# Conditioning products of a four-layer sequence kernel: from split fp32r weights in four columns to unsplit fp32 weights in four column quarters

## The chip, the cores and the metric

The kernel runs on one core of a Trainium2 chip. The metric is device time in microseconds (us) for one execution; the median of three runs before the change is 2190.75 us (2190.43 to 2190.81).

## The reference, cut to what matters

Four blocks transform a sequence of 512 latent tokens with 1024 channels (and, in the first two, 256 context tokens). Before each of the first two layers the input is modulated: a conditioning vector is multiplied by a large weight, and the 3072 results are the layer's shift, scale and gate for each channel. There is one such vector for the latents and one for the context, so the product has only two columns on one side:

```
s = silu(c)                       # [2, 1024]: latents and context
mod = s @ w_ada[l] + b_ada[l]     # [2, 3072], l = 0, 1
shift, scale, gate = split(mod, 3)
h = x * (1 + scale) + shift       # what layer l projects
x = layer_norm(alpha * x + gate * y)
```

Everything else (window attention with a convolution branch in layer 0, a gated linear recurrence in layer 1, then two more blocks with feed-forward networks) is left alone by the change.

## The kernel before

**Layout.** Channels lie on the 128 partitions, in eight tiles; tokens run along the free dimension. A weight is loaded in blocks of 128 x 1024 fp32 (512 KB, all eight k tiles of 128 output channels) by SP's DMA queue into a buffer tagged `r`. ScalarE copies it into a rounded fp32r part `h` (L244), and VectorE or GpSimd subtracts that to get the remainder `l` (L250). A product of a block takes three matmuls for each k tile (L313): high by high, low by high, high by low.

**The conditioning (`conditioning`, `ada`).** The weight `wada` has 2 x 12 chunks of 1 MB. Chunk i below 8 gives shift and scale of channel tile i, chunks 8 to 11 the gates of two tiles each. A chunk comes as two halves (j = 0, 1), each 128 x 1024 with four k tiles of 256 output columns. Here the weight is what *moves* through the array (256 columns at a time) and the conditioning vector `sc` is what stands in it: four columns, latents and context, each in a high and a low part. Each half is split like any other weight, into `h` by ScalarE and `l` by GpSimd (or, in the first stage, by VectorE for j = 1). Then 16 fp32r matmuls (8 k tiles, h and l) add into four partitions of half a PSUM bank. ScalarE copies the 4 x 256 result to `adat_t`; two transposes through the identity (L434) bring it to 128 partitions; VectorE adds the bias and then the low part's result into `mod`.

**First stage, 0 to about 76 us (`layer0`).** For each of the eight channel tiles k: chunk k + 1 is started, chunk k is finished, the input tile x is loaded and modulated on VectorE (`st_g`, two instructions), split into `a_h` (ScalarE) and `a_l` (VectorE), and TensorE runs this tile's products with the first three blocks of `w_ab`. The pool `st` has four `r`, three `h` and three `l` buffers for the chunks. Beside it VectorE and GpSimd prepare the parameters of a later state-space block (`s5_prepare`, tiles `s5t_*` and `s_*`), which a scheduler mixes in by priority.

**Second stage, about 76 to 388 us (`layer0_mix`).** 24 steps of attention (`attend`), each with a block product of `w_ab` woven in, and from `more_ada` one conditioning chunk in each of 16 steps. These halves take their buffers from the common pool `wp`: three `r`, four `h`, four `l`. The last eight chunks' results are layer 1's.

A scheduler orders every engine's instructions when the program is built; each engine then runs its own list strictly in that order. SP's list holds all DMA issues.

Of the kernel before, what the change touches and what calls it, by code (L numbers as in the profile page):

```python
# [10 lines left out]
F32 = mybir.dt.float32  # L11
# [15 lines left out]
# ---------------------------------------------------------------- host layout  # L27


def _blocks(w, kt=None):  # L30
    """[K, M] -> [M/128, 128, K/128 * 128]: block m holds, per partition, all k tiles of 128 columns."""
    k, m = w.shape
    return np.ascontiguousarray(
        w.reshape(k // 128, 128, m // 128, 128).transpose(2, 1, 0, 3).reshape(m // 128, 128, k)
    )


def _col(v):
    """[n*128] -> [128, n]."""
    return np.ascontiguousarray(np.asarray(v).reshape(-1, 128).T)  # L40


def _pair_heads(n):
    """Column order that puts heads j and 4 + j of 64 dims into one tile of 128."""
    return np.concatenate([np.r_[j * 64:(j + 1) * 64, (4 + j) * 64:(5 + j) * 64] for j in range(n // 128)])


def _constants():
    """Tables that depend on shapes alone."""
# [24 lines left out]
    c["steps"] = np.broadcast_to(np.concatenate([np.arange(9), 8 * np.arange(64)]), (128, 73))  # L74
    dm = np.zeros((128, 16))
# [93 lines left out]
# ---------------------------------------------------------------- the program  # L169


class Alloc:
    """A pool of tiles by tag: tags[tag] = (number of buffers, elements per partition)."""
# [14 lines left out]
class Prog:  # L188
    def __init__(self, es, tc, I, off):
# [3 lines left out]
        self.adat = Alloc(es, tc, "adat", {"t": (2, 256)})  # L193
# [26 lines left out]
    def psum(self, **tags):  # L220
        """Shares out the eight banks by tag: those used longest ago first."""
# [20 lines left out]
    # element by element -----------------------------------------------------  # L242
# [25 lines left out]
    # weights ---------------------------------------------------------------  # L268
    def weights(self, ap, n=1024, eng=None, pool=None):
        """A block of a weight, split exactly into two parts of 12 bits."""  # L270
# [17 lines left out]
    def product(self, out, w, xs, cols, k0=0, ks=None):  # L288
        """out = w.T @ x over the k tiles (or some of them), each operand in two parts."""
# [9 lines left out]
    def firsts(self, ps, blocks, xs, tags=("mm",) * 3):  # L299
        """The latents' products of a layer's first blocks in two halves: of three of them tile by tile of xs as these  # L300
        come, then of the others."""
# [13 lines left out]
    # scores of two heads of 64 dims: both parts of a head's queries fill the rows, so that two passes take  # L315
    # (high, low) by high and high by low
# [22 lines left out]
    def out_products(self, ps, block, xs, parts, use, done, keep=3, n=1024, late=(), begun=None, spare=(None, 0)):  # L339
        """The products for all eight tiles of channels; use(m, bank, tokens) takes each. The last `keep` tiles  # L340
        go part by part, done(tokens) follows when all channels of a part are there. The last of xs come late, by these
        numbers; begun: weights and banks of the first three tiles, done up to there."""
# [36 lines left out]
    def rsqrt(self, r0, t, var, eps):  # L379
        """r0 = 1 / sqrt(var + eps), t is scratch: the table's value and one step of Newton's."""  # L380
# [6 lines left out]
    def rsqrt_table(self, p):  # L387
        """Has the table of rsqrt in place from p's time on."""
        self.act(self.dummy, p[:, 0:1], ACT.Abs_reciprocal_sqrt, bias=self.bias[1e-5])
    # conditioning ----------------------------------------------------------  # L390
    def conditioning(self):
# [5 lines left out]
        self.sc = self.const.tile([128, KT, 4], F32R, name="sc")  # L397
        tv = t.rearrange("p (a b) -> p a b", b=2)
        self.copy(self.sc[:, :, 0:2], tv)
        self.sub(self.sc[:, :, 2:4], tv, self.sc[:, :, 0:2].bitcast(F32))  # L400
# [8 lines left out]
    def ada(self, l, i, p, pool=None):  # L409
        """Chunk i of layer l's shift, scale (plus 1) and gate: the shift and scale of channel tile i, or the gates  # L410
        of two tiles; each of the factors in two parts. p: half a bank."""
        for j in range(2):
            eng = self.nc.vector if pool and j else self.nc.gpsimd
            hi, lo = self.weights(self.I["wada"][l * 12 + i][:, j * 1024:(j + 1) * 1024], eng=eng, pool=pool)
            for k in range(4):
                for w in (hi, lo):
                    self.matmul(
                        p[0:4, :], self.sc[:, 4 * j + k, :], w[:, k * 256:(k + 1) * 256], j + k == 0 and w is hi,
                        j == 1 and k == 3 and w is lo,
                    )  # L420

        def copied():
            t = self.adat("t")[0:4, :]
            self.copy(t, p[0:4, :])
            return t
# [3 lines left out]
        def finish(t=t):  # L429
            t = copied() if t is None else t  # L430
            m = slice(i, 16, 8) if i < 8 else slice(2 * i, 2 * i + 2)
            o = p[:, 0:8].rearrange("p (a b c) -> p a b c", a=2, b=2)
            for a in range(2):
                self.nc.tensor.transpose(p[:, 4 * a:4 * a + 4], t[:, a * 128:(a + 1) * 128], self.idn[0:4, 0:4])  # L434
            md = self.mods[l][:, m, :]
            self.add(md, o[:, :, 0], self.bada[:, l, m, :])
            self.add(md, md, o[:, :, 1])
# [3 lines left out]
    # layer 0 ---------------------------------------------------------------  # L441
    def layer0(self, stop=False):
        """Leaves layer 1's modulated inputs in self.a1 and its residual in DRAM."""
        nc, tc = self.nc, self.tc
        mod = self.mods[0]
        with ExitStack() as es:
            a0 = Alloc(es, tc, "a0", {"h": (8, LT), "l": (8, LT)})
# [3 lines left out]
            with ExitStack() as e1:  # L451
                prep = self.s5_open(e3, e1)
                st = Alloc(e1, tc, "st", {"r": (4, 1024), "h": (3, 1024), "l": (3, 1024), "x": (4, LT), "g": (2, LT)})
# [43 lines left out]
            # layer 0's affine map and layer 1's modulation in one  # L497
# [27 lines left out]
    def layer0_mix(self, es, e0, late, xs, Y, first, s5):  # L525
# [33 lines left out]
        def gate(m, pool):  # L559
            """Twice silu."""  # L560
# [30 lines left out]
        def attend(qT, j, n, ctx, y, sg):  # L591
            """Both heads j and 4 + j for one block of 128 queries."""
# [95 lines left out]
        def conv(i):  # L688
            """The four products of a tile of the convolution's channels, one at each step."""
# [57 lines left out]
    def deepnorm(self, N, ps, xr, mod, emit):  # L747
        """xr + gate * out normalized over channels, without the affine map; emit(k, tokens, tile) takes it."""
# [42 lines left out]
    # layer 1 ---------------------------------------------------------------  # L791
    def lower_bounds(self):
        """The gates' lower bounds, and one less them: the softmax over the one layer, its cumulative sum less the
        first term."""
# [44 lines left out]
    def layer1_mix(self, es, K, xs, Y):  # L839
# [13 lines left out]
        def proj(m, ctx):  # L853
            """A product in two steps; returns its banks."""
# [17 lines left out]
        def mixed(t, m, j):  # L872
            """Of [128, n, 2]: token s at index j + (bit of s, by m)."""
            return pattern(t, j, [[4 * m, t.shape[1] // (2 * m)], [2 * m + 1 - 2 * j, 2], [2, m]])

        def across(t, nb, j):
            """Of [128, 2 nb, 2]: the other of each pair, at the same indices."""
            return pattern(t, 2 + j, [[4, nb], [-1 - 2 * j, 2]])

        def project(h):  # L880
            """The head's queries, forget terms and values."""
# [35 lines left out]
        def scan(h):  # L917
# [7 lines left out]
            # the diagonal of the scores, both ways  # L925
# [4 lines left out]
            # the decay of the context's keys  # L930
# [30 lines left out]
            for l in range(7):  # L961
                m = 1 << l
                nb = L // (2 * m)
                # keys of the halves before and after, queries of the others: by the token's bit l
# [14 lines left out]
                # the state from the context  # L979
# [8 lines left out]
            # the states block by block  # L988
# [43 lines left out]
    # the second block ------------------------------------------------------  # L1032
# [833 lines left out]
```

## Time and profile before

| | us |
|---|---|
| median of three runs | 2190.75 |
| the profiled execution, span | 2191.0 |
| TensorE (PE) busy | 2067.3 (94%) |
| VectorE (DVE) busy | 1418.2 (65%) |
| ScalarE (ACT) busy | 953.2 (44%) |
| GpSimd (POOL) busy | 533.7 (24%) |
| SP queue, DMA share of 16 engines | 28.9% |

The profiled execution's span is within 0.3 us of the median. PE's busy time counts a matmul until its result has drained, and matmuls overlap in that; so 94% is not 94% of what PE could do, and the distance between two *starts* in the timeline is what a matmul costs in a row of others. PEclk is the share of its full clock that TensorE was granted.

### The profile page before, as it was taken

Reading aid. Unit: us, or ns where it says so; the run is one execution under the profiler, and the core shown is the slowest. Engines: PE = TensorE matmul, PEld = TensorE weight load, DVE = VectorE, ACT = ScalarE, POOL = GpSimd, SP = SyncE. Lnnn points to the kernel's source line nnn. Section 1 sums busy time; section 2 is a strip of 40 time slices with the busy share of each in tenths; the row PEclk is TensorE's granted clock in tenths of the full one; section 3 lists DMA queues with packets and bytes.
Section 4 is the critical chain, followed back from the end, with each engine's and each line's share of the span. In section 5 each row is a group of like instructions: output and inputs, shape, how many; then the busy total and the mean of one; then the engine's idle time right before and its main releaser. Section 6 shows DMA issues by size and latency. Waiting matters only on the chain.

```text
span 2191.0 us, 29958 instructions
## 1 busy us (share of the span) xinstructions
PE 2067.3 (94%) x11576; PEld 1760.7 (80%) x11576; DVE 1418.2 (65%) x2322; ACT 953.2 (44%) x1681; POOL 533.7 (24%) x442
## 2 busy tenths in 40 slices
PE   5888999999999999998999999999989799999997
PEld 3677878888888888888778888888887588888886
DVE  9885656578666666688665763544579877354455
ACT  4564444345534444435656443222355645322231
POOL 4343433135322222214111320100142333010011
PEclk9999999999999999999998999999999899999998
DMA  7443334132211111133441223332312232323231
GB/s 232 146 141 118 111 113 123 61 121 77 68 49 59 48 49 49 50 115 106 140 126 40 86 86 107 96 97 96 115 39 87 77 106 64 101 96 104 91 108 44
DMA packets 79998, 204.97 MB, mean 94 GB/s; under 512 B 19056, under 2 KB 28016, under 8 KB 79856
## 3 DMA queue, kind: packets, MB, share of 16 engines
q1 hardware_dynamic: 79856, 203.06, 28.9%
q8 instruction: 91, 1.49, 0.3%
q14 instruction: 51, 0.42, 0.1%
HBM read 188.87 MB, written 14.16 MB: 93 GB/s over the span
## 4 chain that ended last, share of the span: by engine, by line
PE 71%; DVE 17%; issue 5%; ACT 4%; POOL 1%; DMA 0%; POOLq 0%; DVEq 0%; SPq 0%; ACTq 0%
PE mm L313 54%; PE a L313 5%; PE mc L313 3%; PE x L313 2%; DVE wp_l L250 1%; DVE res_x L266 1%; PE s L313 1%; PE S L313 1%; PE o L313 1%; ACT wp_h L244 1%; DVE o_a L266 1%; DVE n_a L250 1%; PE z L313 1%; DVE o_xc L266 1%; DVE o_tr L250 1%
## 5 line engine op out<-in xcount | busy, mean ns | idle before, releaser
L244 ACT ACTIVATE wp_h<-wp_r 128x1024 fp32r<-128x1024 f32 (+1 forms) x295 | 303.8, 1039 | 495.3 <-PE mm L313 256.1
L250 DVE TENSOR_TENSOR wp_l<-wp_r,wp_h 128x1024 fp32r<-128x1024 f32 (+1 forms) x236 | 335.1, 1423 | 105.9 <-ACT wp_h L244 105.9
L313 PE MATMUL mm<-act_h,wp_l 128*128 128x512 f32 (+1 forms) x1008 | 379.1, 376 | 12.0 <-DVE wp_l L250 10.2
L313 PE MATMUL mm<-act_h,wp_h 128*128 128x512 f32 (+1 forms) x1008 | 379.8, 377 | 3.3 <-DVE o_xb L250 1.6
L313 PE MATMUL mm<-act_l,wp_h 128*128 128x512 f32 (+1 forms) x1008 | 379.2, 376 | 3.1 <-POOL act_l L250 3.1
L313 PE MATMUL mm<-a_h,wp_h 128*128 128x512 f32 (+1 forms) x920 | 338.8, 369 | 0.4 <-ACT a_h L244 0.4
L313 PE MATMUL mm<-a_l,wp_h 128*128 128x512 f32 (+1 forms) x920 | 331.6, 361 | 1.6 <-DVE a_l L250 1.5
L313 PE MATMUL mm<-a_h,wp_l 128*128 128x512 f32 (+1 forms) x920 | 331.7, 361 | 0.0
L313 PEld LDWEIGHTS mm<-act_h,wp_l 128*128 128x128 f32 x1008 | 193.1, 192 | 46.0 <-DVE wp_l L250 11.1
L313 PEld LDWEIGHTS mm<-act_l,wp_h 128*128 128x128 f32 x1008 | 193.3, 192 | 37.1 <-POOL act_l L250 4.0
L313 PEld LDWEIGHTS mm<-act_h,wp_h 128*128 128x128 f32 x1008 | 193.3, 192 | 37.0 <-ACT wp_h L244 3.8
L250 POOL TENSOR_TENSOR wp_l<-wp_r,wp_h 128x1024 fp32r<-128x1024 f32 x59 | 151.5, 2576 | 225.0 <-ACT wp_h L244 206.8
L313 PEld LDWEIGHTS mm<-a_l,wp_h 128*128 128x128 f32 x920 | 176.3, 192 | 25.9 <-DVE a_l L250 3.3
L250 POOL TENSOR_TENSOR g_g<-g_g,g_u 128x512 f32<-128x512 f32 x44 | 62.2, 1416 | 548.2 <-DVE g_u L250 501.8
L313 PEld LDWEIGHTS mm<-a_h,wp_h 128*128 128x128 f32 x920 | 176.1, 192 | 23.9 <-issue 2.3
L313 PEld LDWEIGHTS mm<-a_h,wp_l 128*128 128x128 f32 x920 | 176.1, 191 | 23.6 <-issue 0.7
L313 PE MATMUL mm<-h_l,wp_h 128*128 128x512 f32 (+1 forms) x344 | 129.2, 376 | 0.6 <-DVE h_l L250 0.5
L313 PE MATMUL mm<-h_h,wp_h 128*128 128x512 f32 (+1 forms) x344 | 129.0, 375 | 0.3 <-ACT h_h L244 0.3
L313 PE MATMUL mm<-h_h,wp_l 128*128 128x512 f32 (+1 forms) x344 | 128.8, 374 | 0.0
L250 DVE TENSOR_TENSOR g_u<-mm,res_rr 128x512 f32<-128x512 f32 x44 | 30.4, 690 | 123.3 <-PE mm L313 123.3
L244 ACT ACTIVATE m_km<-m_k 128x512 f32<-128x512 f32 x56 | 37.6, 672 | 122.7 <-DVE m_k L250 101.0
L313 PEld LDWEIGHTS mm<-h_l,wp_h 128*128 128x128 f32 x344 | 64.8, 188 | 13.6 <-DVE h_l L250 2.1
(505 smaller groups left out, 4117.6 us busy)
## 6 DMA issues: line engine op xcount, KB each, us to landing
wp_r<-w_gu SPq DMA_DIRECT2D x88, 512.0 KB, 3.5
wp_r<-w_c SPq DMA_DIRECT2D x40, 512.0 KB, 3.5
wp_r<-wada SPq DMA_DIRECT2D x32, 512.0 KB, 3.7
wp_r<-w_d SPq DMA_DIRECT2D x32, 512.0 KB, 3.5
wp_r<-w_ab SPq DMA_DIRECT2D x26, 512.0 KB, 4.5
st_r<-wada SPq DMA_DIRECT2D x16, 512.0 KB, 5.5
wp_r<-w_od SPq DMA_DIRECT2D x16, 512.0 KB, 3.5
s_d<-s_s SPq DMA_DIRECT2D x24, 256.0 KB, 2.8
```

The lines of the kernel that those rows point to most:

```text
L244: self.nc.scalar.activation(out=out, in_=in_, func=ACT.Copy, scale=scale)
L250: (eng or self.nc.vector).tensor_tensor(out=out, in0=a, in1=b, op=op)
L266: self.nc.vector.scalar_tensor_tensor(out=out, in0=a, scalar=s, in1=b, op0=op0, op1=op1)
L313: self.nc.tensor.matmul(out=out, lhsT=a, rhs=b, start=start, stop=stop)
```

## The change

`sc` becomes 128 x 8 x 32 fp32: the two vectors unsplit, and 30 columns of zeros. A chunk's weights are no longer split: the raw fp32 half moves. Of the four k tiles in a half, tile k goes through columns 32k to 32k + 31 of the array and adds into partitions 32k to 32k + 31 of the bank, so that a chunk takes 8 fp32 matmuls: two in each quarter, the second accumulating on the first. ScalarE now copies 128 x 256. Two fp32 matmuls with a 0/1 matrix `sel` (128 x 2, ones where the partition's number modulo 32 is 0 or 1) take the place of the transposes: they turn the result and sum the four quarters. One add of the bias remains. The pool `st` has six `r` buffers and no `h`, `l`. `conditioning` moved into `layer0`, so that its tiles are freed with the layer.

```diff
-        self.sc = self.const.tile([128, KT, 4], F32R, name="sc")
+        self.sc = cond.tile([128, KT, 32], F32, name="sc")
+        self.nc.gpsimd.memset(self.sc, 0.0)
         tv = t.rearrange("p (a b) -> p a b", b=2)
-        self.copy(self.sc[:, :, 0:2], tv)
-        self.sub(self.sc[:, :, 2:4], tv, self.sc[:, :, 0:2].bitcast(F32))
+        self.nc.vector.tensor_copy(out=self.sc[:, :, 0:2], in_=tv)
+        self.sel = cond.tile([128, 2], F32, name="sel")
+        self.nc.sync.dma_start(out=self.sel, in_=self.I["sel"])
...
     def ada(self, l, i, p, pool=None):
+        raw = []
         for j in range(2):
-            eng = self.nc.vector if pool and j else self.nc.gpsimd
-            hi, lo = self.weights(self.I["wada"][l * 12 + i][:, j * 1024:(j + 1) * 1024], eng=eng, pool=pool)
+            t = (pool or self.wp)("r")
+            self.nc.sync.dma_start(out=t, in_=self.I["wada"][l * 12 + i][:, j * 1024:(j + 1) * 1024])
+            raw.append(t)
+        for j in range(2):
             for k in range(4):
-                for w in (hi, lo):
-                    self.matmul(
-                        p[0:4, :], self.sc[:, 4 * j + k, :], w[:, k * 256:(k + 1) * 256], j + k == 0 and w is hi,
-                        j == 1 and k == 3 and w is lo,
-                    )
+                self.nc.tensor.matmul(
+                    out=p[32 * k:32 * k + 32, :], lhsT=self.sc[:, 4 * j + k, :],
+                    rhs=raw[j][:, k * 256:(k + 1) * 256], start=j == 0, stop=j == 1, tile_position=(0, 32 * k),
+                )
...
-            t = self.adat("t")[0:4, :]
-            self.copy(t, p[0:4, :])
+            t = self.adat("t")
+            self.copy(t, p)
...
-            o = p[:, 0:8].rearrange("p (a b c) -> p a b c", a=2, b=2)
+            o = p[:, 0:4].rearrange("p (a c) -> p a c", a=2)
             for a in range(2):
-                self.nc.tensor.transpose(p[:, 4 * a:4 * a + 4], t[:, a * 128:(a + 1) * 128], self.idn[0:4, 0:4])
-            md = self.mods[l][:, m, :]
-            self.add(md, o[:, :, 0], self.bada[:, l, m, :])
-            self.add(md, md, o[:, :, 1])
+                self.matmul(o[:, a], t[:, a * 128:(a + 1) * 128], self.sel)
+            self.add(self.mods[l][:, m, :], o, self.bada[:, l, m, :])
...
-                st = Alloc(e1, tc, "st", {"r": (4, 1024), "h": (3, 1024), "l": (3, 1024), "x": (4, LT), "g": (2, LT)})
+                st = Alloc(e1, tc, "st", {"r": (6, 1024), "x": (4, LT), "g": (2, LT)})
```

TensorE, first stage, before: the end of the second chunk's run and the start of the next (`st_h`, `st_l` are a half's two parts, `t` the half bank, `mm` and `c` products of `w_ab`).

```order
L313 MATMUL t<-st_h,sc 4x256
L313 MATMUL t<-st_l,sc 4x256
L434 MATMUL t<-idn,adat_t 128x4 x2
L313 MATMUL t<-st_h,sc 4x256
L313 MATMUL mm<-a_h,wp_h 128x512
L313 MATMUL t<-st_l,sc 4x256
```

TensorE, the start of its list now:

```order
L425 MATMUL t<-st_r,sc 32x256 x8
L313 MATMUL t<-sel,adat_t 128x2 x2
L425 MATMUL t<-st_r,sc 32x256 x8
L313 MATMUL t<-sel,adat_t 128x2 x2
L313 MATMUL mm<-a_h,wp_h 128x512
L313 MATMUL mm<-a_l,wp_h 128x512
L313 MATMUL c<-a_h,wp_h 128x256
```

The first two chunks now stand whole at the head of the list, straight behind their loads; from the third on each half is a run of four between the products of earlier tiles.

GpSimd, first stage, before: subtractions of half chunks (`st_l`) between those products of the parameter preparation that run there (`s_w`).

```order
L1183 MEMSET s5t_z 128x128
L250 TENSOR_TENSOR st_l<-st_r,st_h 128x1024 x2
L250 TENSOR_TENSOR s_w<-s5t_u,s5t_steps 128x288
L250 TENSOR_TENSOR st_l<-st_r,st_h 128x1024 x3
L250 TENSOR_TENSOR s_w<-s5t_w,s5t_t 128x512
```

GpSimd, the same place now:

```order
L1190 MEMSET s5t_z 128x128
L250 TENSOR_TENSOR s_w<-s5t_u,s5t_steps 128x288
L250 TENSOR_TENSOR s_w<-s5t_w,s5t_t 128x512 x2
L250 TENSOR_TENSOR s_w<-s5t_u,s5t_steps 128x512
L250 TENSOR_TENSOR m_sh<-m_sh,m_sin 128x512
```

The eight subtractions are gone, and the first work of the second stage (`m_sh`) stands right behind the preparation's.

SP's DMA list in the second stage with what each issue waits for, before (`w_ab` a block of the layer's weight, `wada` a half chunk; the names in brackets are semaphores of the DMA queues and of the engine that releases the buffer):

```order
L273 DMA wp_r<-wada 128x1024 [waits DMAHW5_49,Pool_49]
L273 DMA wp_r<-wada 128x1024 [waits Pool_49]
L273 DMA wp_r<-w_ab 128x1024 [waits DMAHW7_49,DMAHW3_49,DVE_49]
L1268 DMA rope_d<-s5t_w 128x512 [waits DMAHW0_49,DVE_49]
L1267 DMA rope_d<-s5t_w 128x512 [waits DMAHW1_49,Activation_49]
```

SP's list now, at the same step:

```order
L421 DMA wp_r<-wada 128x1024 [waits DMAHW6_49,DMAHW2_49,DVE_49]
L421 DMA wp_r<-wada 128x1024 [waits DMAHW7_49,PE_49]
L273 DMA wp_r<-w_ab 128x1024 [waits DMAHW1_49,DMAHW0_49,PE_49]
L1278 DMA s_d<-s_s 128x512 [waits DVE_49]
L1278 DMA s_d<-s_s 128x512 [waits Activation_49]
```

A raw buffer that held a half chunk used to be released by GpSimd's subtraction; it is now released by TensorE's matmuls on it, and the next block of `w_ab` waits for that. Behind about 388 us the instructions of every engine stand in the same order as before.

More of the change, by code (lines that the diff above doesn't have):

```diff
@@ L74, in _constants @@
     c["steps"] = np.broadcast_to(np.concatenate([np.arange(9), 8 * np.arange(64)]), (128, 73))
+    c["sel"] = np.tile(np.eye(32, 2), (4, 1))
     dm = np.zeros((128, 16))
@@ L192, in __init__ @@
         self.const = es.enter_context(tc.tile_pool(name="const", bufs=1))
-        self.adat = Alloc(es, tc, "adat", {"t": (2, 256)})
         self.wp = Alloc(es, tc, "wp", {"r": (3, 1024), "h": (4, 1024), "l": (4, 1024)})
@@ L389, in rsqrt_table, with conditioning @@
         self.act(self.dummy, p[:, 0:1], ACT.Abs_reciprocal_sqrt, bias=self.bias[1e-5])
-    def conditioning(self):
+    def conditioning(self, es):
+        cond = es.enter_context(self.tc.tile_pool(name="cond", bufs=1))
+        self.adat = Alloc(es, self.tc, "adat", {"t": (2, 256)})
         cv = self.vec("cvec")
@@ L444, in layer0 @@
         nc, tc = self.nc, self.tc
-        mod = self.mods[0]
         with ExitStack() as es:
+            self.conditioning(es)
+            mod = self.mods[0]
             a0 = Alloc(es, tc, "a0", {"h": (8, LT), "l": (8, LT)})
@@ L1815, in dump @@
                 result(k, X)
-        P.conditioning()
         if start == 0:
```

## Prediction

> **What bounds the kernel now.** First the windows, cut where the work changes: first stage, second, and the rest, whose order the change leaves alone. Columns: length, busy time of PE, PEld, DVE, ACT and POOL, granted clock, DMA share, GB/s.
>
> ```profile
> 0.00:76.00 76.00, 50.12 (x278) 33.72 (x279) 67.10 (x165) 34.40 (x50) 27.03 (x28) 1.00 0.67 222
> 76.00:388.00 312.00, 281.33 (x1828) 239.75 (x1826) 215.43 (x468) 154.13 (x333) 119.71 (x80) 0.96 0.38 119
> 388.00:2191.00 1803.00, 1735.85 (x9475) 1487.20 (x9474) 1135.68 (x1690) 764.70 (x1300) 386.92 (x334) 0.98 0.26 84
> ```
>
> Only the first 388 of 2191 us can change. In the first stage VectorE is busy 67.1 of 76 us; in the second TensorE is the bound, idle 30.7 of 312, and a mean clock of 0.96 says that it ran at half for some 25 us, worth 12 more. Second view, what TensorE waited for: three rows of the first stage, three of the second (total, times, longest).
>
> ```profile
> PE t L313 <- ACT st_h L244: 12.4, 3, 10.6
> PE t L313 <- DVE st_l L250: 6.5, 5, 2.0
> PE t L313 <- POOL st_l L250: 4.8, 4, 2.1
> ...
> PE x L313 <- DVE m_T L647: 14.4, 5, 4.0
> PE pt L588 <- ACT m_q L244: 5.4, 1, 5.4
> PE pt L654 <- DVE m_T L647: 5.3, 5, 1.3
> ```
>
> First it waits for the splitting of `wada`, later for copies, 25.1 us in these three. Why VectorE is late there shows in the timeline: POOL's subtractions of two half chunks, and VectorE at that time.
>
> ```profile
> 147.80 5.92 POOL L250 TENSOR_TENSOR wp_l<-wp_r,wp_h 128x1024 fp32r<-128x1024 f32 x2
> ...
> 151.38 2.36 DVE L250 TENSOR_TENSOR m_st<-m_st 128x2 f32<-128x2 f32 x1
> ...
> 154.33 0.16 DVE L250 TENSOR_TENSOR m_st<-vecs,m_st 128x2 f32<-128x2 f32 x1
> ```
>
> An operation on two columns takes 2.36 us beside POOL's and 0.16 after it: VectorE stood still for 2.2.
>
> **Part 1: the splitting goes.** The subtractions of the first stage (count, ns min/median/max), and the window of stage two on `wp_l` alone (PE, PEld, DVE, POOL):
>
> ```profile
> L250 POOL TENSOR_TENSOR st_l<-st_r,st_h x8: 2354/2492/3227, 10.6 to 59.9; 128x1024 fp32r<-128x1024 f32 x8
> L250 DVE TENSOR_TENSOR st_l<-st_r,st_h x8: 1210/1218/3372, 13.4 to 65.4; 128x1024 fp32r<-128x1024 f32 x8
> ...
> 76.00:388.00 312.00, 138.20 (x436) 71.52 (x436) 34.58 (x21) 81.24 (x32) 0.96 0.38 119
> ```
>
> In stage one VectorE loses 8 subtractions (about 12 us) and up to 8 x 2.2 us of standing still: 67 falls to 38. In stage two POOL loses 81 of 120 us, and VectorE up to 32 x 2.2 = 70 of 215. That is worth only the waiting above and the half clock that follows pauses: bounds 0 and 25 + 12 = 37 us. I take 20, over half, because VectorE then has much slack but products still wait for chains of softmax steps.
>
> **Part 2: the matmuls.** One chunk in the TensorE timeline, its first, second and last matmul and what follows:
>
> ```profile
> 145.24 0.28 PE L313 MATMUL mc<-wp_h,sc 128*4 128x256 f32 x1 [1.79 <-DVE mod L250]
> 145.36 0.28 PE L313 MATMUL mc<-wp_l,sc 128*4 128x256 f32 x1
> ...
> 146.96 0.28 PE L313 MATMUL mc<-wp_l,sc 128*4 128x256 f32 x1
> 147.07 0.60 PE L644 MATMUL pt<-idn,m_P 128*128 128x128 f32 x4
> ```
>
> A start every 0.115 us, a chunk 1.83 us. No row has an fp32 matmul in a column quarter; the nearest is fp32 in the whole array with 512 columns:
>
> ```profile
> 1272.36 1.02 PE L313 MATMUL z<-res_acc,ones 128*128 128x512 f32 x2
> 1272.82 0.79 PE L313 MATMUL mm<-act_h,wp_h 128*128 128x512 f32 x1
> 1273.45 0.39 PE L313 MATMUL mm<-act_l,wp_h 128*128 128x512 f32 x1
> ```
>
> The program has one matmul there and the trace two records: fp32 runs as two passes, one behind the other. The next fp32r product needs 0.23 us and ends about 1273.45, so the two took 0.86: 0.43 for 512 columns, 0.215 for 256. A chunk now has 16 such passes. Bounds: all in a row 16 x 0.215 = 3.44 us; all four quarters at once 4 x 0.215 = 0.86. Between them: TensorE's records start in the order of the list, so the second pass of a quarter, which needs the same columns as the first, stands ahead of the next quarter's first pass; only second and next first overlap. Eight matmuls then take 9 x 0.215 = 1.94 us, in two runs of four 2.15. I take this value: it is what two passes in one quarter and starts in order give, if quarters are independent at all. The Trainium skill ("TensorEngine Tiling (Array Packing)", Key Properties) speaks against the change: switching the tiling mode drains TensorE. Here the 4-column matmul at 146.96 is followed by a full-width one 0.11 us later, so no drain is seen in this trace. By the rule, with a drain estimated as the 0.28 us of a matmul less its 0.115, stage two's 16 chunks would lose two each, 5 us, and the sum would be 2172; by the row it is nothing, and the sum stays with the row.
>
> The turn: the transposes before, and small fp32 matmuls with a 128-column weight, the nearest to the two with `sel` (four records).
>
> ```profile
> 49.90 0.28 PE L434 MATMUL t<-idn,adat_t 4*128 4x4 f32 x2
> 50.11 0.39 PE L313 MATMUL c<-a_h,wp_h 128*128 128x256 f32 x1
> ...
> 150.04 1.45 PE L313 MATMUL x<-m_vn,m_T 128*128 128x64 f32 x12
> 151.29 0.48 PE L313 MATMUL mm<-a_h,wp_l 128*128 128x512 f32 x1
> ```
>
> 0.21 us becomes 4 x 1.25 / 12 = 0.42. A chunk thus costs TensorE +0.32 us (+1.82 in a row, -0.76 at once), in stage two 16 times: +5 (+29, -12). With the 20 us of part 1: **stage two -15 us**.
>
> **Part 3: the first stage.** Its landmarks: both halves of the first chunk landed, the first `mod`, first and last `a_h`; a chunk's matmuls early on; the DMA at its best; one tile's products with one block.
>
> ```profile
> 9.45 1.06 ACT L244 ACTIVATE st_h<-st_r 128x1024 fp32r<-128x1024 f32 x1 [1.06 <-DMA st_r<-wada]
> 10.73 1.06 ACT L244 ACTIVATE st_h<-st_r 128x1024 fp32r<-128x1024 f32 x1 [0.22 <-DMA st_r<-wada]
> ...
> 24.88 0.83 ACT L244 ACTIVATE a_h<-st_g 128x768 fp32r<-128x768 f32 x1
> ...
> 66.97 0.84 ACT L244 ACTIVATE a_h<-st_g 128x768 fp32r<-128x768 f32 x1 [2.00 <-DVE st_g L263]
> ...
> 22.11 0.15 DVE L250 TENSOR_TENSOR mod<-mod,t 128x4 f32<-128x4 f32 x1
> ...
> 13.17 0.42 PE L313 MATMUL t<-st_h,sc 128*4 128x256 f32 x1
> 13.38 0.42 PE L313 MATMUL t<-st_l,sc 128*4 128x256 f32 x1
> ...
> 12.00:16.00 4.00, 1.87 (x8) 0.86 (x8) 4.00 (x4) 2.34 (x2) 3.45 (x2) 1.00 1.00 387
> ...
> 70.57 0.69 PE mm L313 x3
> 71.25 0.35 PE c L313 x3
> ```
>
> Early TensorE starts one pass per 0.21 us, half speed. Now the first chunk's passes begin at 9.45: two runs of 5 x 0.43 end at 13.8; copy 0.4, `sel` 0.8, add 0.2: `mod` at 15.2 instead of 22.3, **-7 us**. From then on a tile takes (66.97 - 24.88) / 7 = 6.0 us. New floors per tile: DMA 1.44 MB at 387 GB/s 3.7 us; VectorE 38 / 8 = 4.8; TensorE three blocks x (0.69 + 0.35) + 2.15 + 0.42 = 5.7. TensorE sets the pace, and the seven tiles gain 7 x 0.3 = **2 us**. The tail behind the last `a_h` stays. Stage one: **-9 us**.
>
> **What is moved at no cost.** In stage two a buffer of `wada` is now released by TensorE, and the next `w_ab` block and SP's stores queue behind that wait. Cover: between that chunk and the block's first product TensorE's list holds 27,700 columns or more, at 0.115 us per 256 over 12 us.
>
> ```profile
> wp_r<-w_ab SPq DMA_DIRECT2D x26, 512.0 KB, 4.5
> L244 ACT ACTIVATE wp_h<-wp_r 128x1024 fp32r<-128x1024 f32 (+1 forms) x295 | 303.8, 1039 | 495.3 <-PE mm L313 256.1
> L250 DVE TENSOR_TENSOR wp_l<-wp_r,wp_h 128x1024 fp32r<-128x1024 f32 (+1 forms) x236 | 335.1, 1423 | 105.9 <-ACT wp_h L244 105.9
> ```
>
> Landing 4.5, copy 1.0 and subtraction 1.4 need 7; without cover a step would lose the difference. The wider copy of `adat_t` has the same 256 columns per partition; memset, `sel` load and `sc` copy lie ahead of the first landing.
>
> **Sum.** -9 - 15 = -24 us on the profiled 2191.0, which is the median within 0.3: **2167 us**. A measurement here can tell 0.2%, 4.4 us, from no change.
>
> **Rivals.**
> - *Slower: quarters wait for each other.* If the array takes one fp32 pass at a time whatever its columns, a chunk costs 3.44 us. Stage two: +29 - 20 = +9. Stage one: first `mod` 16 x 0.43 + 1.4 after 9.45, at 17.7, -4; the pace is 3.1 + 3.4 + 0.4 = 7.0 us, +7; together +3. **2203 us.** For it: no row shows two matmuls streaming at once. Against: nothing in the trace either, since all matmuls of before that are 32 columns wide stand in the same quarter. It decides from about 3 us per chunk on, where the total crosses zero.
> - *Faster: all four at once.* If a quarter's second pass waits without holding up the others, a chunk takes 0.86 us. Stage two -12 - 20 = -32; stage one: `mod` at 14, -8, then VectorE's 4.8 us is the pace, -9. **2142 us.** The Trainium skill ("TensorE: Matmul & The Clock Gate", Part 3) gives starts about 4 ns apart for matmuls in different tiles and 2.38 times the rate for three column tiles, and also says that matmuls start and end strictly in order; no run here shows either for fp32.
> - *VectorE's freedom buys little.* Stage two's waits may be the softmax chain itself: then 20 shrinks towards 0 and my forecast becomes 2187. This is inside the range.
>
> **How the numbers follow.** Overlap by halves 0.47, in a row 0.31, all at once 0.22. The range reaches from the fast case with a few us more of part 1 to the slow one with a few us less: **2138 to 2206**, about 0.1 outside at each end. The forecast's own range is 2154 to 2189. Faster by over 0.2%: 0.45 + 0.22 + 0.03 = 0.70; within: 0.06; slower: 0.24.
>
> **What would show it.** Starts of the eight records' pairs in a chunk: every 0.215 us in a row (16 starts over 3.4 us), in pairs (1.9), or nearly together (0.9). VectorE's 2.36 us rows gone, m_T waits below 10 us, first `mod` near 15 us, last `a_h` near 58. The prediction is wrong if a chunk takes over 3 us, if waits of `mm` for `wp_l` or `wp_h` appear in stage two, or if the time behind stage two changes by more than 3 us.

## The result, and the profile after

The changed kernel takes 2130.2 us (median of four runs, 2128.3 to 2134.4) beside 2190.6 of the kernel before: a ratio of 0.973, 95% interval 0.972 to 0.975. That is 60 us less, where 24 were forecast, and below the range's 2138. A second set of runs gave 2130.7 and the ratio 0.973 again (0.972 to 0.975). The profiled execution's span is 2132.6 us, against 2191.0.

To compare two traces, cut both at the same piece of work and not at the same time. The first cut here is the first transpose of `m_q`, where stage two's attention begins; the second is the first split of stage two's results, `a_h<-y_y`. Windows of the kernel before, cut there (length; PE, PEld, DVE, ACT, POOL; granted clock, DMA share, GB/s):

```profile
0.00:88.29 88.29, 57.04 (x310) 39.19 (x311) 77.20 (x172) 41.37 (x59) 36.78 (x34) 0.99 0.66 218
88.29:439.17 350.88, 325.58 (x2132) 279.13 (x2133) 237.37 (x553) 167.81 (x385) 117.38 (x80) 0.97 0.34 108
439.17:2191.00 1751.83, 1684.68 (x9136) 1442.35 (x9134) 1103.64 (x1597) 744.05 (x1239) 379.50 (x328) 0.98 0.26 84
```

The same windows of the changed kernel:

```profile
0.00:73.41 73.41, 54.04 (x331) 36.45 (x331) 49.20 (x157) 25.00 (x41) 10.59 (x25) 0.98 0.69 239
73.41:379.12 305.71, 304.69 (x2161) 259.74 (x2162) 195.76 (x537) 142.08 (x356) 38.31 (x50) 1.00 0.41 130
379.12:2132.60 1753.48, 1687.07 (x9136) 1443.96 (x9134) 1104.88 (x1597) 743.92 (x1239) 378.15 (x328) 0.98 0.27 84
```

Stage one gave 14.9 us, stage two 45.2, and the rest took 1.6 us more. In stage two TensorE's idle time fell from 25.3 us to 1.0 (length less PE), its busy time by 20.9, and its clock is whole. What TensorE still waits for there (total, times, longest) shows the first of these from the other side:

```profile
PE pt L595 <- ACT m_q L244: 0.9, 1, 0.9
PE S L313 <- DVE m_qs L250: 0.4, 1, 0.4
PE pt L651 <- ACT m_T L244: 0.3, 1, 0.3
PE mc L425 <- DVE mod L250: 0.2, 1, 0.2
```

Of the 25.1 us in the three largest waits before, 1.2 are left. A chunk in TensorE's timeline, with the instruction behind it:

```profile
132.22 1.07 PE L425 MATMUL mc<-wp_r,sc 128*32 128x256 f32 x16 [0.20 <-DVE mod L250]
133.22 0.66 PE L651 MATMUL pt<-idn,m_P 128*128 128x128 f32 x4
```

Sixteen records (two passes for each of eight fp32 matmuls), and the next matmul starts 1.00 us after the first of them: not 3.44, not 1.94. The starts of the single records of this chunk in the trace, in ns from its first:

```
0 7 13 21 | 240 247 253 261 | 456 462 469 477 | 672 678 685 692
```

Four records start 7 ns apart, and the next four 0.216 to 0.240 us later: the passes of all four quarters stream at once.

Landmarks of stage one, after: the first `mod`, the first and the last `a_h`.

```profile
15.18 0.16 DVE L250 TENSOR_TENSOR mod<-t,bada 128x4 f32<-128x4 f32 x1 [3.15 <-PE t L313]
...
19.86 0.84 ACT L244 ACTIVATE a_h<-st_g 128x768 fp32r<-128x768 f32 x1 [2.48 <-DVE st_g L263]
...
59.96 0.85 ACT L244 ACTIVATE a_h<-st_g 128x768 fp32r<-128x768 f32 x1 [1.21 <-DVE st_g L263]
```

And the last `a_h` of the kernel before:

```profile
71.42 0.85 ACT L244 ACTIVATE a_h<-st_g 128x768 fp32r<-128x768 f32 x1 [2.07 <-DVE st_g L263]
```

The row at 66.97, which the prediction called the last, is the seventh of eight. From first to last the pace was (71.42 - 24.88) / 7 = 6.65 us a tile, and is now 5.73.

### The profile page after: what moved, and what is told of

Read it like the earlier page. It is cut to its first block, busy times and chain, and to the rows that moved or that the text cites. A ratio compares the mean times of both kernels' runs of the same rounds, so it can differ in the third digit from the quotient of the medians.

```text
span 2132.6 us, 29872 instructions
## 1 busy us (share of the span) xinstructions
PE 2045.8 (96%) x11624; PEld 1740.2 (82%) x11624; DVE 1349.8 (63%) x2290; ACT 911.0 (43%) x1634; POOL 427.0 (20%) x403
## 4 chain that ended last, share of the span: by engine, by line
PE 76%; DVE 13%; issue 5%; ACT 4%; POOL 1%; DMA 1%; SPq 0%; POOLq 0%; DVEq 0%; ACTq 0%
PE mm L313 56%; PE a L313 5%; PE mc L313 3%; PE x L313 2%; PE S L313 2%; DVE res_x L266 1%; PE s L313 1%; PE pt L651 1%; PE o L313 1%; DVE wp_l L250 1%; PE mc L425 1%; DVE o_xc L266 1%; DVE n_a L250 1%; ACT wp_h L244 1%; PE z L313 1%
## 5 line engine op out<-in xcount | busy, mean ns | idle before, releaser
L244 ACT ACTIVATE wp_h<-wp_r 128x1024 fp32r<-128x1024 f32 (+2 forms) x263 | 271.3, 1037 | 456.1 <-PE mm L313 263.4
L250 DVE TENSOR_TENSOR wp_l<-wp_r,wp_h 128x1024 fp32r<-128x1024 f32 (+1 forms) x236 | 326.9, 1388 | 108.7 <-ACT wp_h L244 108.6
L250 POOL TENSOR_TENSOR wp_l<-wp_r,wp_h 128x1024 fp32r<-128x1024 f32 x27 | 69.4, 2574 | 135.9 <-ACT wp_h L244 119.0
```

The source lines that it names most:

```text
L244: self.nc.scalar.activation(out=out, in_=in_, func=ACT.Copy, scale=scale)
L250: (eng or self.nc.vector).tensor_tensor(out=out, in0=a, in1=b, op=op)
```

## The experiments

The theory after the result: quarters stream side by side, and the splitting (not the matmuls) made most of the waits, because VectorE stands still while GpSimd subtracts. Rivals: the gain is all matmul time; or the splitting hurt through ScalarE's copies, or through GpSimd's own lateness. All experiments start from the changed kernel. Stage one is the time to the first `pt<-idn,m_q`, stage two that from there to the first `a_h<-y_y`; VectorE and GpSimd are busy times in stage two; all in us. The ratio is to the kernel before in the same set of runs, with its 95% interval.

| kernel | median | ratio | stage one | stage two | VectorE | GpSimd |
|---|---|---|---|---|---|---|
| before | 2190.6 | | 88.3 | 350.9 | 237.4 | 117.4 |
| changed | 2130.2 | 0.972-0.975 | 73.4 | 305.7 | 195.8 | 38.3 |
| changed, second set | 2130.7 | 0.972-0.975 | 72.2 | 305.3 | 194.6 | 38.7 |
| one quarter | 2182.9 | 0.996-0.998 | 80.6 | 349.9 | 195.2 | 37.7 |
| two quarters | 2148.4 | 0.979-0.984 | 74.7 | 322.5 | 196.2 | 39.7 |
| pairs in the list | 2139.3 | 0.975-0.979 | 76.1 | 310.8 | 195.6 | 38.7 |
| dead splitting | 2170.0 | 0.989-0.994 | 86.7 | 333.2 | 230.6 | 112.1 |
| dead subtractions | 2152.6 | 0.980-0.984 | 81.0 | 319.8 | 221.5 | 98.3 |
| dead copies | 2128.4 | 0.969-0.973 | 71.4 | 307.2 | 197.1 | 39.1 |
| dead scalar products | 2145.7 | 0.977-0.981 | 77.1 | 317.1 | 206.2 | 123.8 |
| dead subtractions, two tiles | 2164.0 | 0.986-0.990 | 84.5 | 324.8 | 228.4 | 112.0 |
| dead copies and scalar products | 2153.1 | 0.980-0.986 | 77.9 | 322.5 | 203.5 | 124.5 |
| short scalar products | 2127.4 | 0.970-0.973 | 68.6 | 305.7 | 194.7 | 50.6 |
| dead splitting on VectorE | 2144.4 | 0.977-0.981 | 74.0 | 316.5 | 237.6 | 44.4 |
| some splits to VectorE | 2126.7 | 0.968-0.972 | 71.7 | 306.2 | 194.9 | 38.5 |
| all splits to VectorE | 2107.6 | 0.961-0.965 | 72.4 | 306.8 | 195.4 | 38.5 |

"Dead" work is issued and never read.

### What streams beside what

**One quarter, and two.**

```diff
+                c = 32 * (k % Q)          # Q = 1 or 2 instead of 4
-                    out=p[32 * k:32 * k + 32, :], ... start=j == 0, stop=j == 1, tile_position=(0, 32 * k),
+                    out=p[c:c + 32, :], ... start=4 * j + k < Q, stop=4 * j + k >= 8 - Q, tile_position=(0, c),
```

The copy to `adat_t` and the `sel` products take only the 32 or 64 partitions that are then used.

> All eight fp32 matmuls of a chunk go through the first 32 columns, the rest as in the changed kernel. Theory (quarters stream side by side, passes of one quarter one behind the other): a chunk takes 16 passes x 0.215 = 3.44 us instead of 4 x 0.216, +2.6 in each of 16 steps of stage two = +41, and in stage one a tile's pace goes from 5.1-5.7 to 7.0 us and the first mod comes about 3 us later, +12 to +15; total 2180 to 2190. Rival (the records are short for another reason, fp32 with 32 columns being cheap): chunk stays near 1 us, total 2130 within 4.

> The k tiles share two quarters, four k tiles each. Theory: a chunk's matmuls take 8 x 0.215 = 1.73 us, almost the 1.83 of the kernel before, so what is left of the gain is what the splitting cost: stage two +0.86 x 16 = +14 against the changed kernel, stage one +2 to +5, total 2145 to 2150, i.e. some 42 us of the 60 remain. Rival (the gain is matmul time): with the chunk back at the old length the gain is nearly gone, 2180 or more.

TensorE's timeline with one quarter:

```profile
131.21 3.64 PE L426 MATMUL mc<-wp_r,sc 128*32 128x256 f32 x16 [0.24 <-DVE mod L250]
134.78 0.33 PE L652 MATMUL pt<-idn,m_P 128*128 128x128 f32 x1
```

With two quarters:

```profile
120.64 1.92 PE L426 MATMUL mc<-wp_r,sc 128*32 128x256 f32 x16
122.49 0.55 PE L652 MATMUL pt<-idn,m_P 128*128 128x128 f32 x3
```

From the first start to that of the next instruction a chunk takes 3.57, 1.85 and, with four quarters, 1.00 us: 16, 8 and 4 passes of 0.216 in a row, plus 0.1. Both totals fell where the theory put them (2182.9, 2148.4). With two quarters a chunk is as long as it was before the change (1.83), and 42 of the 60 us are still there. So going from two quarters to four is worth 18 us, and the gain isn't all matmul time.

**Pairs in the list.** Both k tiles of a quarter stand next to each other.

```diff
-        for j in range(2):
-            for k in range(4):
+        for k in range(4):
+            for j in range(2):
                 self.nc.tensor.matmul(
```

> The list has the two k tiles of a quarter next to each other: q0 q0 q1 q1 q2 q2 q3 q3 instead of q0 q1 q2 q3 twice. Theory A (each quarter has its own turn, a waiting pass does not hold up other quarters): starts still in groups of four every 0.216 us, chunk about 1.0 us, total 2130 within 4. Theory B (passes start in the order of the list, one that waits for its quarter holds up those behind): a matmul's second one waits for its own quarter, only the last pass of one quarter overlaps the next: 13 x 0.215 = 2.8 us a chunk, total 2165 to 2175.

A whole chunk's 16 starts, in ns, with this list:

```
0 13 31 44 | 240 253 271 284 | 456 469 486 500 | 671 685 702 716
```

Still four at a time. A quarter's second matmul is second in the list, ahead of the other quarters' first, and yet the three starts behind the first come 13 to 44 ns after it, when that quarter is still streaming. The records don't name their quarter; but within one quarter, passes come 0.216 us apart, so these three can only be those of the other quarters. They now lie 13 to 18 ns apart instead of 7. Where the list is cut after two matmuls by a `sel` turn, the difference shows in the timeline:

```profile
235.50 1.05 PE L425 MATMUL mc<-wp_r,sc 128*32 128x256 f32 x4
236.48 0.61 PE L313 MATMUL mc<-sel,adat_t 128*128 128x2 f32 x4
237.02 1.08 PE L425 MATMUL mc<-wp_r,sc 128*32 128x256 f32 x12
238.03 0.44 PE L651 MATMUL pt<-idn,m_P 128*128 128x128 f32 x2
```

Two matmuls of one quarter take 0.98 us to the next instruction, and the other six, of three quarters, 1.01. Theory A holds for the streaming, and theory B's 2.8 us a chunk and 2165 to 2175 are ruled out. But theory A's total was missed: 2139.3 is 9 us over the 2130 it gave. In stage two, 5.1 us longer, TensorE is idle 4.3 us instead of 1.0 and busy 1.8 more; in stage one, 2.7 us longer, each chunk's first pair stands alone, with other products between it and the rest. Why the waits in stage two grew was not followed up.

### What the splitting cost

**The whole splitting, dead.**

```diff
             raw.append(t)
+            hi, lo = self.parts_of(pool or self.wp)
+            self.copy(hi, t)
+            self.sub(lo, t, hi.bitcast(F32), self.nc.vector if pool and j else self.nc.gpsimd)
...
-    "r": (6, 1024),
+    "r": (4, 1024), "h": (3, 1024), "l": (3, 1024),
```

> The changed kernel with the old splitting issued beside it, its results unused: ScalarE's copy to h and GpSimd's (in stage one for j = 1 VectorE's) subtraction to l for each half, buffers as before. Theory (VectorE, held up by GpSimd's subtractions, caused the waits): the long VectorE rows of 2.4 us come back, TensorE's idle time in stage two goes back towards 30 us; only the matmuls' 13 us less 3 for the turn and part of stage one remain: 2165 to 2180. Rival (the gain is matmul time, VectorE had slack): 2130 to 2138.

```profile
0.00:86.74 86.74, 57.66 (x336) 38.82 (x336) 75.51 (x165) 41.93 (x59) 38.03 (x35) 0.95 0.65 215
86.74:419.91 333.17, 315.13 (x2156) 266.61 (x2157) 230.62 (x537) 170.54 (x386) 112.14 (x80) 0.97 0.36 116
```

40 us come back, 13.3 in stage one and 27.5 in stage two, and TensorE is idle 18.0 us again. VectorE has the same 537 instructions in stage two as without the dead work, and is busy 230.6 us instead of 195.8. The comparison with the kernel before is the other half of it: with the splitting still there, the rest of the change gains 20 us (1.6 and 17.7 by stage). That is not matmul time alone: the products no longer wait for the parts, every engine's list stands in another order, and in stage two TensorE is idle 7.3 us less and busy 10.5 us less.

**Its halves.** Subtractions alone, then copies alone (with six `r` buffers in stage one).

```diff
+            lo = (pool or self.wp)("l", dt=F32R)
+            self.sub(lo, t, t, self.nc.vector if pool and j else self.nc.gpsimd)
```

```diff
+            hi = (pool or self.wp)("h", dt=F32R)
+            self.copy(hi, t)
```

> The changed kernel with only the subtractions of the old splitting beside it, on the raw half and with unused results: GpSimd (two tensor operands, 128 x 1024; in stage one VectorE for j = 1), no copies on ScalarE. Theory (VectorE stands still while GpSimd subtracts): most of the 40 us that all of the splitting cost come back, 2155 to 2170. Rival (ScalarE's 32 to 48 copies of 1.06 us and the chain copy - subtraction - product cost it): 2130 to 2140.

> The changed kernel with only ScalarE's copies of the raw halves beside it, results unused. Theory: ScalarE, busy 142 of 306 us in stage two, has room: 2130 to 2137. Rival (the copies stood in front of the softmax's exponentials and of the copies that TensorE waits for): 2150 or more.

Copies are free (2128.4). The subtractions alone cost 22 us: too much for the copies to be the cause, and below the 25 to 40 that the theory wanted. With the same tile as both operands GpSimd's instruction took 1.96 us instead of 2.46, so the test was weaker than meant. It was made again with two different tiles:

```diff
+            v = lambda a: a.rearrange("p (a b) -> p a b", b=128)
+            o = self.idn.unsqueeze(1).to_broadcast([128, 8, 128])
-            self.sub(lo, t, t, self.nc.vector if pool and j else self.nc.gpsimd)
+            self.sub(v(lo), v(t), o, self.nc.vector if pool and j else self.nc.gpsimd)
```

> As the kernel with dead subtractions, but the second operand is another tile (the identity, repeated over the columns) instead of the raw half itself: with the same tile twice GpSimd's subtraction took 1.99 us instead of 2.46 and VectorE's long rows came to 0.8 us each instead of 1.4. Theory (what VectorE loses beside the subtraction sets the cost): the subtraction is back at about 2.4 us, VectorE loses 1.4 beside each, and the time goes from 2153 towards the 2170 of the whole dead splitting, 2160 to 2170. Rival (the whole splitting costs more since GpSimd also waits for ScalarE's copy and its later work with it): stays at 2150 to 2156.

2164.0, as the theory had it: 34 of the 40 us come from the subtractions.

**GpSimd as busy, VectorE free.** Times a constant instead of minus a tile, first without the copies, then on the copy, with the whole chain.

```diff
-            self.sub(lo, t, t, self.nc.vector if pool and j else self.nc.gpsimd)
+            if pool and j:
+                self.sub(lo, t, t)
+            else:
+                self.ts(lo, t, 0.5, ALU.mult, eng=self.nc.gpsimd)
```

> As the kernel with dead subtractions, but GpSimd's instruction is one tensor times a constant (same 128 x 1024 in, same out) in place of a difference of two tensors; VectorE's own dead subtractions in stage one stay. In this trace GpSimd's tensor-times-scalar rows (m_k, 128 x 512, 25.6 us in all) lie beside VectorE work that is no longer than usual, its two-tensor rows beside VectorE work that is. Theory (only the two-tensor form holds VectorE up): GpSimd is as busy as with the subtractions, VectorE's long rows are not there, 2132 to 2143. Rival (GpSimd's own queue came late, whatever it ran): as with the dead subtractions, 2155 or more.

> As the kernel with the whole dead splitting (ScalarE's copies, buffers and chain as before the change), but GpSimd multiplies the copy by a constant instead of subtracting two tensors. Theory (VectorE held up by the two-tensor form): VectorE's excess beside GpSimd falls by two thirds and 12 to 25 us of the 40 go, 2145 to 2158, though GpSimd is busy longer (2.9 us each). Rival (GpSimd's queue, late through its own length and its wait for the copy, is all): 2170 or more.

Timeline of the kernel with the whole dead splitting, GpSimd and VectorE at one time:

```profile
189.05 2.77 POOL L250 TENSOR_TENSOR wp_l<-wp_r,wp_h 128x1024 fp32r<-128x1024 f32 x1 [0.22 <-ACT wp_h L244]
...
189.47 2.37 DVE L266 SCALAR_TENSOR_TENSOR m_st<-m_st,m_s 128x2 f32<-128x2 f32 x1
```

Timeline of the kernel with dead copies and scalar products, the same kind of place (the first row is two instructions in line):

```profile
186.76 6.14 POOL L263 TENSOR_SCALAR wp_l<-wp_h 128x1024 fp32r<-128x1024 f32 x2 [6.53 <-ACT wp_h L244]
...
188.23 0.16 DVE L266 SCALAR_TENSOR_TENSOR m_st<-m_st,m_s 128x2 f32<-128x2 f32 x1
188.43 0.16 DVE L250 TENSOR_TENSOR m_st<-vecs,m_st 128x2 f32<-128x2 f32 x1
```

Two columns on VectorE take 2.37 us beside GpSimd's difference of two tensors, and 0.16 in the middle of its scalar product. The windows of stage two say the same, first without the copies:

```profile
77.05:394.19 317.14, 309.55 (x2161) 263.69 (x2162) 206.17 (x537) 139.34 (x354) 123.83 (x80) 0.98 0.39 124
```

and with them:

```profile
77.87:400.34 322.47, 311.15 (x2156) 266.88 (x2157) 203.49 (x537) 170.89 (x386) 124.50 (x80) 0.97 0.38 120
```

VectorE loses 8 to 10 us instead of 35, with GpSimd busy 12 us longer than with the subtractions. With the copies the total (2153.1) is where the theory had it, without them (2145.7) it lies between the theory's 2143 and the rival's 2155. Either way a cost of 15 to 23 us remains: of the 40 us, VectorE's standing still accounts for 17 (2170.0 less 2153.1), or more, since GpSimd is busier with the scalar products; and GpSimd, busy as it is, does harm in another way too. The traces point to one: in stage two, SP's list, which holds all loads, waits for GpSimd's own later copies to `s5t_w` (parts of the preparation that are to be stored) for 14.7 us with the scalar products, 16.7 with copies and scalar products and 14.8 with the whole dead splitting, but not at all in the changed kernel. That this wait makes the loss was not tested.

**What else on GpSimd, and VectorE with the load alone.** The scalar product on 64 columns instead of 1024; and the whole dead splitting with VectorE doing all of it.

```diff
-                self.ts(lo, t, 0.5, ALU.mult, eng=self.nc.gpsimd)
+                self.ts(lo[:, 0:64], t[:, 960:1024], 0.5, ALU.mult, eng=self.nc.gpsimd)
```

```diff
-            self.sub(lo, t, hi.bitcast(F32), self.nc.vector if pool and j else self.nc.gpsimd)
+            self.sub(lo, t, hi.bitcast(F32))
```

> As the kernel with GpSimd's dead tensor-times-constant instructions, which still cost 15 us without holding VectorE up much, but each on 64 columns instead of 1024: GpSimd still stands in line for each half's load, and is busy for a few tenths of a us instead of 2.86. If GpSimd's time in the instruction made its later work late: 2131 to 2137. If its standing behind the load of a half did: 2143 to 2148.

> The whole dead splitting with every subtraction on VectorE, none on GpSimd. VectorE's busy time in stage two should be about 195 + 32 x 1.2 = 233 us, as in the dead splitting with GpSimd (230.6), and GpSimd's as in the changed kernel. If VectorE's lost time sets the cost: 2160 to 2172. If GpSimd's late queue carries its share of about 15 us: 2145 to 2157.

Stage two of the first:

```profile
68.56:374.30 305.74, 304.41 (x2161) 259.77 (x2162) 194.69 (x537) 142.60 (x357) 50.62 (x80) 1.00 0.41 130
```

and of the second:

```profile
74.01:390.47 316.46, 307.83 (x2151) 262.28 (x2152) 237.64 (x584) 168.68 (x385) 44.41 (x53) 0.98 0.39 124
```

Short instructions that stand in line for the same loads cost nothing (2127.4, below both expectations), so it was GpSimd's time in the instruction (SP's wait for `s5t_w` is 2.3 us there). VectorE with more work than it lost in standing still (237.6 us busy) costs 14 us, not 40; the value lies just below the lower of the two expectations. Stage one is then back at 74.0 us, though all the splitting is done, with the same buffers as in the dead splitting.

### A version that beats both

If 2.5 us on GpSimd cost VectorE more than the 1.2 us that a subtraction takes there, the splits of weights that GpSimd still does should move.

```diff
-        ws = [self.weights(b, eng=self.nc.gpsimd) for b in blocks]
+        ws = [self.weights(b) for b in blocks]
-  ([self.weights(block(m), n, self.nc.gpsimd) for m in range(3)], ...
+  ([self.weights(block(m), n) for m in range(3)], ...
```

> The changed kernel, with most of those splits of weights that GpSimd still does (first products of a layer, first three blocks of an output projection) given to VectorE. Theory: a subtraction costs VectorE 1.2 us of its own in place of some 2.1 us of standing still, so VectorE gains about 0.9 us each, but behind stage two TensorE is busy 1736 of 1753 us, so little of it shows: 2124 to 2132. Rival (VectorE's time there is not spare, and GpSimd's subtractions were hidden): 2134 or more.

2126.7: inside the theory's bounds, but the intervals of the two ratios overlap, so it is not told apart from the changed kernel. Then the recurrent block's too:

```diff
-            w = self.weights(self.I["w_od"][m], eng=eng or nc.gpsimd)
+            w = self.weights(self.I["w_od"][m], eng=eng)
-            w = self.weights(self.I["w_rg"][b], eng=nc.gpsimd)
+            w = self.weights(self.I["w_rg"][b])
```

> The changed kernel with all splits of weights that GpSimd still does given to VectorE (the first products of a layer, output projections, and the recurrent block's weights as well). By the theory VectorE gains about 0.9 us for each, TensorE's waits behind stage two (10 us for wp_l, 10.5 for po_a) shrink a little: 2120 to 2128. Rival (in the recurrent block VectorE is the late engine): 2130 or more.

> The changed kernel once more beside the others on this chip, as the measure for differences of a few us: 2128 to 2134.

2107.6 us, ratio 0.963 (0.961 to 0.965): 23 us below the changed kernel on the same chip, and more than expected. What follows stage two, in the changed kernel of that set:

```profile
377.55:2129.40 1751.85, 1683.62 (x9136) 1441.20 (x9134) 1104.56 (x1597) 743.96 (x1239) 378.00 (x328) 0.98 0.27 84
```

and with the splits on VectorE:

```profile
379.16:2103.30 1724.14, 1674.16 (x9136) 1433.41 (x9134) 1084.11 (x1624) 744.83 (x1239) 312.86 (x301) 0.99 0.27 86
```

VectorE has 27 more instructions and is busy 20 us less; TensorE is idle 50.0 us instead of 68.2, at a slightly higher clock.

## Why the prediction was wrong

**The failed step: two passes in line.** "The second pass of a quarter, which needs the same columns as the first, stands ahead of the next quarter's first pass; only second and next first overlap." The starts show otherwise: a pass that waits for its own quarter doesn't hold up those of other quarters, with the list in either order. The chunk takes 1.00 us, not 1.94: 16 x 0.94 = 15 us in stage two. The reason given, that records start in the order of the list, was read off a trace in which every matmul used the same columns or all of them, so it could not show the difference. The mechanism of the rival of all four at once was right, and so was its 0.86 us for four passes in a row.

The two stages were missed by 36 us. Part 1 is 7.5 of them, part 3 is 6, and the other 23 are what stage two gained without the splitting's cost: -17.7 us (stage two before, against that of the dead splitting) where +5 was forecast. In these 23 are the 15 us of the failed step; the turn through `sel`, 0.53 us instead of 0.42, takes 2 back. The remaining 9.5 are no work on the chunks: against the kernel before, a chunk and its turn save 16 x 0.51 = 8 of the 17.7 us, and most of the rest is the 7.3 us by which TensorE is idle less. Why it is idle less there stays open. The rival's 2142 is too high for the same reasons: it took 20 us for the splitting, too, and nothing for these waits.

**Part 1, the splitting in stage two: right in kind, mis-sized, and its mechanism only half of it.** 20 us were taken between 0 and 37; the dead splitting costs 27.5. The wait rows named VectorE, and VectorE did stand still. But scalar products on GpSimd, beside which VectorE loses only 10 us, cost 11.4 us there, and the load of all the splitting on VectorE 10.8. The bound counted the waits that the rows show and the half clock, and it held.

**Part 3, stage one: -14.9 instead of -9.** The first `mod` came when it was forecast (15.2, -7), but by luck. Two runs of four matmuls, each 2.15 us, were reckoned from 9.45 on. They take half of that, and the halves landed later:

```profile
10.09 1.08 PE L425 MATMUL t<-st_r,sc 128*32 128x256 f32 x8 [10.09 <-DMA st_r<-wada]
12.48 1.08 PE L425 MATMUL t<-st_r,sc 128*32 128x256 f32 x8 [1.31 <-DMA st_r<-wada]
```

The old pace was taken from a row that isn't the last `a_h`; it was 6.65 us and not 6.0. That the new mean, 5.73, is the forecast's 5.7 is luck again. The steps from one `a_h` to the next are 10.5, 8.8, 3.2, 5.3, 5.1, 5.1 and 2.1 us, which is no steady pace, and the 5.7 counted 2.15 + 0.42 us for a chunk that TensorE does in 0.57 + 0.57 + 0.36 near 52 us. There, from 45 to 60 us, TensorE is busy without a gap, as the forecast had it, but at 5.1 us a tile. The 14.9 us are made up of 5.0 up to the first `a_h`, 6.4 over the seven steps, where 2 were forecast, and 3.4 behind the last one (16.9 us before, 13.5 now), where the prediction said that the tail stays. Why the tail is shorter was not followed up. By the experiments TensorE isn't what the old stage waited for: with the new matmuls and the old splitting it is 86.7 us long. It was GpSimd, since with the same splitting on VectorE it is 74.0.

**The drain.** The prediction saw none. A loss of that kind is there, but small. TensorE's timeline of the changed kernel, where a chunk stands between other matmuls:

```profile
228.93 0.28 PE L313 MATMUL mc<-a_l,wp_h 128*128 128x256 f32 x1
229.05 0.28 PE L313 MATMUL mc<-a_h,wp_l 128*128 128x256 f32 x1
229.26 0.63 PE L425 MATMUL mc<-wp_r,sc 128*32 128x256 f32 x6
229.82 0.61 PE L313 MATMUL mc<-sel,adat_t 128*128 128x2 f32 x4
230.35 1.05 PE L425 MATMUL mc<-wp_r,sc 128*32 128x256 f32 x10
```

From 229.05 to the chunk's first start are 0.21 us instead of 0.12: 0.09 lost on the way in, and about as much on the way out (the last four starts of the whole chunk come by 0.69, a pass needs 0.216, and the next matmul starts at 1.00). That is some 0.2 us a chunk, 3 us over stage two. The rule of the Trainium skill ("TensorEngine Tiling (Array Packing)", Key Properties), that changing the tiling mode drains TensorE, agrees. With one quarter the loss on the way out is the same 0.09 us, so it belongs to the 32-column matmuls and not to four of them at once. The row that the prediction set against the rule, a 4-column matmul with a full-width one 0.11 us behind it, shows no loss at all, so it could not speak for these 32-column matmuls. The `sel` turn takes 0.53 us with the switch behind it, where 0.42 was reckoned.

**What was right.** The end of the 2.36 us rows (the longest instruction on two columns that VectorE has in stage two is now 1.24 us), `m_T` waits below 10 us (0.3), no wait of `mm` for a weight in stage two, and nothing behind stage two (1.6 us). The last `a_h` near 58 (59.96) came out of the errors of part 3, which made up for each other.

## What to carry to other kernels

When several matmuls have few columns of the stationary operand, give each its own column quarter: the time goes by the busiest quarter, and within an unbroken run not by the order of the list. But put different quarters next to each other in it all the same: where a run is cut, a pair of one quarter stands alone, and the kernel with pairs took 9 us longer, though its waits were not followed up. Before giving work to an idle GpSimd, look at what VectorE's smallest instructions take beside it: a subtraction of two tensors there can cost VectorE twice what it would take on VectorE itself. And where a trace has no case that tells two mechanisms apart, as here for quarters, no order of instructions in it is a reason to prefer one.

## What the runs showed of the hardware

- fp32 matmuls of 32 columns in four quarters: starts 7 ns apart, one pass 0.216 us for 256 columns, two passes a matmul; a chunk 3.57, 1.85 and 1.00 us in one, two and four quarters. The Trainium skill ("TensorE: Matmul & The Clock Gate", Part 3) gives about 4 ns between starts and a rate of 2.38 for three column tiles; here it is 3.6 for four. It also says that matmuls start strictly in order; with the list in pairs the starts here don't follow the list.
- GpSimd holds VectorE up when it reads two tensors, hardly when it reads one: 2.37 against 0.16 us for two columns. The Trainium skill ("SBUF — State Buffer", SBUF: two separate sides) has a shared port pair, locked for a whole instruction by a GpSimd operation that reads SBUF against a VectorE one with two inputs. The two-tensor runs agree; the scalar products read SBUF too, and two-input instructions of VectorE ran their 0.16 us in the middle of them. In the kernel with copies and scalar products, 20 of 23 such two-column instructions took at most 0.16 us, the longest 1.00; in the middle of the dead splitting's subtractions there are five, and none took under 1.18.
- Left open: stage one of the kernel with short scalar products is 68.6 us long, below the 72 to 73 of the changed kernel, with more work in it.
